# Attention probabilities turned by VectorE in 32x32 blocks, values in eight tiles of TensorE: one layer of a hybrid backbone

## The chip, the cores and the metric

The kernel runs on one core of a Trainium2 chip. The core has five engines with instruction streams of their own: TensorE (PE: matmuls and, ahead of each, a weight load, PEld), VectorE (DVE), ScalarE (ACT), GpSimd (POOL) and SyncE (SP, which here only issues DMAs). They wait for one another through semaphores. An engine works through its stream in order, so an instruction that waits holds everything behind it on that engine. The metric is the device time of one execution in microseconds (us). A profile of one execution shows every instruction with start and duration.

## The reference

One layer for 128 context tokens and 512 latent tokens, width 1024, 16 query heads of 64 in 4 groups that each share one key and value head, all in float32. The part that matters here:

```python
q = rms_norm(q.reshape(B, N, N_HEADS, HEAD_DIM), p["q_norm"])
...
keys = jnp.concatenate([ctx_k, apply_axial_rope(k, rope_tabs)], axis=1)
vals = jnp.concatenate([ctx_v, v], axis=1)
...
s = jnp.einsum('bqkgd,btkd->bkgqt', qblk, k) * scale
p = jax.nn.softmax(s, axis=-1)
o = jnp.einsum('bkgqt,btkd->bqkgd', p, v)
```

Latent queries read 128 cached and 512 new keys (640 in all), context queries the 128 context keys. The rest of the layer (modulation "ada", projections, a gated convolution, two output products, a feed-forward part) surrounds this.

## The kernel before

Tokens lie in tiles of 128 rows. Large products are made of three float32r matmuls, high and low parts of both operands (mm3, L157 to L159); the high part of a weight is a rounded copy, the low part the difference ("cut"). [...]

**The loop.** The attention runs over four head groups g, and in each over nine steps i: step 0 takes the context queries with all four heads, steps 1 to 8 take one tile of 128 latent queries and two heads each. A step has these parts:

- scores (L589): twelve matmuls, the two heads side by side in two row tiles of 64 partitions, into two PSUM buffers of 1024 columns; three of these exist (tag s2), taken in a ring.
- maxima per head on VectorE (L727), multiplied by the query's norm factor (L729); exponential with row sum on ScalarE (L742); reciprocal on VectorE (L751); shares (probabilities) on GpSimd, one multiply for each head (L752).
- The probabilities of the step before are turned on TensorE, ten 128x128 transposes against an identity (L765), and copied out of PSUM by ScalarE or VectorE (L770).
- After two steps of the same head pair, the values (L789): ten matmuls, two column tiles at once, keys on the partitions, 256 query columns moving. The result leaves as a high part (AH, ScalarE, L794) and a low part (AL, VectorE, L795). The context step's values are L780.

**What fills the steps.** Between these parts TensorE projects the queries of later tiles (q_part, 24 matmuls of mm3, in two halves), VectorE and GpSimd rotate them (L517 to L525), ScalarE squares them (L529) and VectorE and GpSimd make the norm factors (L535 to L537). q_turn (L560) transposes a finished query tile; its high part goes to ScalarE (L563) and its low part to VectorE (L566). In some steps a product of the modulation weights (ada, L209; its sum is folded by VectorE, L230) is made, and the weights that come next are cut (CUTS; high on ScalarE L690, low on VectorE L693). In the last group the projection of a gate takes the place of the queries' (gate_part).

**What sets the order.** The order on each engine is that of the program text, written out by hand in the loop. SP's queue loads raw weights by a ring: each use of a piece lets the next be fetched. Small results (query projections, query turns, ada, values) use ps1: two tiles of one PSUM bank each, taken in turn. Each of them is its own tile, so that a writer waits only for the readers of that one.

Of the kernel before, what the change touches and what calls it, by code (L numbers as in the profile page):

```python
# [14 lines left out]
ALU = mybir.AluOpType  # L15
# [46 lines left out]
def trunk_layer(ctx, tc, x_prompt, x_sample, cache_k, cache_v, c, c_ctx, w_ada, b_ada, g_pre1, g_post1, g_pre2,  # L62
# [25 lines left out]
    psa = single.enter_context(tc.tile_pool(name="psa", bufs=2, side="right", space=bass.MemoryType.PSUM))  # L88
# [12 lines left out]

    def ps1():
        return psa.tile([128, 512], F32, tag="s1", name=nm("s1"), bufs=2)
# [84 lines left out]
    bct = dp.tile([64, 128], F32, name="bct")  # L188
    hd = dp.tile([NT, 128, D], F32, name="hd")
# [75 lines left out]
    with tc.tile_pool(name="pro", bufs=2) as pro, tc.manual_schedule(engines={mybir.EngineType.SP}):  # L265
# [122 lines left out]
        VV = kvp_.tile([128, 6, 256], F32, name="VV")  # L388
# [59 lines left out]
        for f in range(KT):  # L448
# [7 lines left out]
            if f == 2:  # L456
                nc.sync.dma_start(VV[:, 0, :], cache_v.rearrange("t h d -> t (h d)"))
# [51 lines left out]
    with tc.tile_pool(name="att", bufs=2) as at:  # L509
        def wide(shape, s="pr"):  # L510
            return at.tile(shape, F32, tag="pr", name=nm(s), bufs=4)
# [30 lines left out]
        def q_begin(g):  # L542
            rq[g] = at.tile([128, NT, 4], F32, tag="rq", name=nm("rq"), bufs=2)

            QH[g], QL[g] = (at.tile([128, 2, NTOK], F32R, tag=x, name=nm(x), bufs=2) for x in ("QH", "QL"))
# [11 lines left out]
        def q_turn(g, t, p=None):  # L557
            p = ps1() if p is None else p
            for i in range(2):
                PE.transpose(p[:, i * 128:(i + 1) * 128], qfs[g, t][:, 2 * i:2 * i + 2].rearrange("p h d -> p (h d)"), ident)  # L560
            src = p[:, 0:256].rearrange("p (i c) -> p i c", i=2)
            qh, ql = (x[g][:, :, t * 128:(t + 1) * 128] for x in (QH, QL))
            S.activation(qh, src, AF.Copy)  # L563

            def low():
                V.tensor_tensor(out=ql, in0=src, in1=qh.bitcast(F32), op=ALU.subtract)  # L566
            return low

        def q_turn_both(g):

            p = ps2()
            for t in range(2):
                for i in range(2):
                    PE.transpose(p[:, 512 * t + i * 128:512 * t + (i + 1) * 128], qfs[g, t][:, 2 * i:2 * i + 2].rearrange("p h d -> p (h d)"),
                                 ident)
            src = p.rearrange("p (t i c) -> p i t c", t=2, c=128)[:, 0:2]
            qh, ql = (x[g][:, :, 0:256].rearrange("p i (t c) -> p i t c", t=2) for x in (QH, QL))

            def parts():
                S.activation(qh, src, AF.Copy)  # L580
                V.tensor_tensor(out=ql, in0=src, in1=qh.bitcast(F32), op=ALU.subtract)
            return parts

        def scores(outs, g, pi, qs, kh, kl, ks):

            for n, (kk, q) in enumerate(((kh, QH[g]), (kl, QH[g]), (kh, QL[g]))):
                for h in range(2):
                    rows = slice(64 * h, 64 * h + 64)
                    PE.matmul(outs[h], q[rows, pi, qs], kk[rows, g, ks], start=n == 0, stop=n == 2, tile_position=(64 * h, 0))  # L589
# [11 lines left out]
        ring = ada_raws(0, 1) + [("u", 10), ("u", 11)] + ada_raws(1, 4) + [("u", 12)] + ada_raws(4, 5) + [("u", 13)] + ada_raws(5, 8)  # L601
        ring += [("u", 14)] + ada_raws(8, 9) + [("u", 15)] + ada_raws(9, 12) + [("u", 16)] + ada_raws(12, 15) + [("u", 17)]
        ring += ada_raws(15, 16) + [("u", 18)]
# [28 lines left out]
        def k_rotate(t):  # L632
            if t in (0, 2):
                room = wide([128, 2, NKV, HD], "room")
                kf, tm = room[:, 0], room[:, 1]
                kds[t] = wide([128, NKV, 2, HD], "room")
            else:
                room = at.tile([128, 5, 256], F32, tag="PT", name=nm("room"), bufs=3)
                kf, tm = (room[:, i, :].rearrange("p (h d) -> p h d", d=HD) for i in range(2))
                kds[t] = room[:, 2:4, :].rearrange("p a (b s d) -> p (a b) s d", s=2, d=HD)  # L640
# [4 lines left out]
        def k_copies(t):  # L645
            sqs[t] = squares(kvp[t][:, 0:256])
            S.activation(VV[:, 5 if t == 0 else t, :], kvp[t][:, 256:512], AF.Copy)
# [4 lines left out]
        def k_double(t):  # L652
# [6 lines left out]
            if t == 0:  # L659
                nc.sync.dma_start(new_v.rearrange("t h d -> t (h d)"), VV[:, 5, :])  # L660
# [20 lines left out]
        PT = {}  # L681

# [3 lines left out]
        def cut_hi(i):  # L686
# [4 lines left out]

            def low(a=0, b=1024):
                V.tensor_tensor(out=lo[:, a:b], in0=raw[:, a:b], in1=hi[:, a:b].bitcast(F32), op=ALU.subtract)  # L693
                if b == 1024:
                    ring_used(1)
            state["cut"].append(Unit((hi, lo), units[i][4]))
            return low

        class Step:


            def __init__(self, g, place=None):
                self.g, self.place = g, place
                self.ctx = place is None
                self.pr = {}
                if self.ctx:
                    p = ps2().rearrange("p (h i c) -> p h i c", h=2, c=128)
                    for i in range(2):
                        scores([p[:, h, i, :] for h in range(2)], g, i, slice(0, 128), KCH, KCL, slice(0, 128))
                    self.sc = p[:, :, 0:2, :].rearrange("p h i c -> p i h c")  # L710
                else:
                    qh, pi, qi = place
                    q0 = NCTX + qh * 256 + qi * 128
                    both = [ps2(), ps2()]
                    for b0, b1 in BLKS:
                        scores([x[:, OFF + b0:OFF + b1] for x in both], g, pi, slice(q0, q0 + 128), KH, KL, slice(b0, b1))
                    self.sc = [x[:, OFF:OFF + NTOK] for x in both]

            def most(self, h):
                if self.ctx:  # L720
                    self.mx = small("mxc", 4, 1)
                    V.tensor_reduce(out=self.mx.rearrange("p (i h) -> p i h", h=2), in_=self.sc, axis=AX.X, op=ALU.max, negate=True)
                    V.tensor_tensor(out=self.mx, in0=self.mx, in1=rq[self.g][:, 0, :], op=ALU.mult)
                    return
                qh, pi, qi = self.place
                mx = small("mx")
                V.tensor_reduce(out=mx, in_=self.sc[h], axis=AX.X, op=ALU.max, negate=True)  # L727
                rs = rq[self.g][:, 1 + 2 * qh + qi, 2 * pi + h:2 * pi + h + 1]
                V.tensor_tensor(out=mx, in0=mx, in1=rs, op=ALU.mult)  # L729
                self.pr[h] = (mx, rs)  # L730

            def exps(self, h):
                if self.ctx:
                    pr, self.sm = at.tile([128, 4, 128], F32, tag="pr", name=nm("pr"), bufs=4), small("smc", 4, 1)
                    for i in range(4):
                        S.activation(pr[:, i, :], self.sc[:, i // 2, i % 2, :], AF.Exp, bias=self.mx[:, i:i + 1],
                                     scale=rq[self.g][:, 0, i:i + 1], accum_out=self.sm[:, i:i + 1])
                    self.pr = pr
                    return
                mx, rs = self.pr[h]  # L740
                pr, sm = wide([128, NTOK]), small("sm")
                S.activation(pr, self.sc[h], AF.Exp, bias=mx, scale=rs, accum_out=sm)  # L742
                self.pr[h] = (pr, sm)

            def shares(self, h):
                if self.ctx:
                    V.reciprocal(self.sm, self.sm)
                    G.tensor_tensor(out=self.pr, in0=self.pr, in1=self.sm.unsqueeze(2).broadcast_to((128, 4, 128)), op=ALU.mult)
                    return
                pr, sm = self.pr[h]  # L750
                V.reciprocal(sm, sm)  # L751
                G.tensor_tensor(out=pr, in0=pr, in1=sm.broadcast_to((128, NTOK)), op=ALU.mult)  # L752
                self.pr[h] = pr

            def turned(self, h):

                p = ps2()
                if self.ctx:
                    for i in range(4):
                        PE.transpose(p[:, i * 128:(i + 1) * 128], self.pr[:, i, :], ident)  # L760
                    dst = PT[self.g, "c"] = at.tile([128, 4, 128], F32, tag="PT", name=nm("PT"), bufs=3)
                    return lambda: S.activation(dst, p[:, 0:512].rearrange("p (h c) -> p h c", c=128), AF.Copy)
                qh, pi, qi = self.place
                for k in range(5):
                    PE.transpose(p[:, k * 128:(k + 1) * 128], self.pr[h][:, k * 128:(k + 1) * 128], ident)  # L765
                if qi == 0:
                    PT[self.g, qh, pi, h] = at.tile([128, 5, 256], F32, tag="PT", name=nm("PT"), bufs=3)
                dst = PT[self.g, qh, pi, h][:, :, qi * 128:(qi + 1) * 128]
                src = p[:, 0:640].rearrange("p (k c) -> p k c", c=128)
                return lambda v=False: V.tensor_copy(dst, src) if v else S.activation(dst, src, AF.Copy)  # L770

        def values(g, pair=None):

            vcol = slice(g * HD, (g + 1) * HD)
            pv = ps1()
            if pair is None:
                pt = PT.pop((g, "c"))
                for h in range(4):
                    o = 64 * (h % 2)
                    PE.matmul(pv[o:o + 64, (h // 2) * 128:(h // 2) * 128 + 128], VV[:, 5, vcol], pt[:, h, :], start=True, stop=True,  # L780
# [1197 lines left out]
```

## Time and profile before

| what | us |
|---|---|
| median of 3 runs | 1136.38 |
| lowest and highest | 1134.15, 1136.91 |
| span of the profiled execution | 1134.1 |
| first latent scores of group 0 | 77.03 |
| values of step 4 of groups 0, 1, 2, 3 begin | 96.04, 145.90, 195.76, 245.30 |
| last values of the attention | 278.9 to 281.3 |

TensorE is busy for 1114.9 us of the span (98%), VectorE for 796.3, ScalarE for 569.9 and GpSimd for 158.9. In the profile "busy" adds the durations of an engine's instructions; matmuls are pipelined, so their ends are modelled. A group of instructions is told by its line, engine, operation and tiles ("out<-in"), with count, busy time and the mean in ns, and behind the bar the idle time just ahead of them with what ended it. The chain of waits is the list of pieces followed back from the end: each is what released the next. The profile's lines bear the kernel's line numbers (L765), and "128*64" is the shape of the tile of TensorE's array. The attention stretch is about 206 us of the 1134.1; what comes after it (convolution, output and feed-forward products, mostly L1030) is the same text in both kernels.

### The profile page before, as it was taken

To read this page: it belongs to the slowest core of one execution; us is meant where nothing else is said; L and a number is where in the kernel's file an instruction comes from. 1 tells how busy PE (TensorE), PEld (TensorE's weight loads), DVE (VectorE), ACT (ScalarE), POOL (GpSimd) and SP (SyncE) were. 2 spreads that over 40 slices of the span, in tenths; PEclk is the share of its full clock that TensorE was granted. 3 is DMA by queue.
4 is the path that set the end of the run, shared out by engine and by line. 5 is a ranking of instruction groups with operands and counts; after the bars stand their busy time and mean duration, and the time that the engine had idled before them with its cause. 6 is when DMAs were issued, how large, how long until landed. Compare 5 with 4: busy or idle time off the path is not lost.

```text
span 1134.1 us, 19512 instructions
## 1 busy us (share of the span) xinstructions
PE 1114.9 (98%) x7885; PEld 1024.5 (90%) x7885; DVE 796.3 (70%) x1269; ACT 569.9 (50%) x979; POOL 158.9 (14%) x198
## 2 busy tenths in 40 slices
PE   7999999999999999999999999999999999999997
PEld 6787888888999999999999889999999999998786
DVE  4587666654656798889645458888788778888544
ACT  4375666665234444545522256655554545555431
POOL 2056566652000000000000012000000000002001
PEclk9999999999999999999999999999999999999999
DMA  9632433333222223223332644233333323315732
GB/s 335 205 92 82 126 94 112 110 96 112 76 75 75 75 77 105 81 75 95 93 111 76 207 164 150 76 99 99 98 112 109 95 91 109 105 61 186 240 99 93
DMA packets 177304, 129.58 MB, mean 114 GB/s; under 512 B 6274, under 2 KB 159422, under 8 KB 177214
## 3 DMA queue, kind: packets, MB, share of 16 engines
q1 hardware_dynamic: 177102, 128.30, 36.4%
q8 instruction: 62, 1.02, 0.4%
q14 instruction: 28, 0.23, 0.1%
q10 hardware_dynamic: 112, 0.04, 0.0%
HBM read 116.87 MB, written 11.45 MB: 113 GB/s over the span
## 4 chain that ended last, share of the span: by engine, by line
PE 89%; DVE 3%; ACT 1%; POOL 0%; issue 0%; DVEq 0%; POOLq 0%; ACTq 0%
PE b L1030 45%; PE b L159 9%; PE b L157 9%; PE b L158 9%; PE s L789 3%; PE s L765 3%; PE s L589 3%; PE s L157 2%; PE s L159 2%; PE s L158 2%; PE s L209 1%; DVE Y L1514 1%; DVE wlo L693 0%; PE s L560 0%; PE b L1421 0%; DVE mx L727 0%
## 5 line engine op out<-in xcount | busy, mean ns | idle before, releaser
L1030 PE MATMUL b<-ZB,whi 128*128 128x322 f32 x1024 | 228.6, 310 | 0.0
L1030 PEld LDWEIGHTS b<-ZB,whi 128*128 128x128 f32 x1024 | 173.8, 189 | 1.6
L1030 PE MATMUL b<-ZB,wlo 128*128 128x322 f32 x512 | 159.4, 311 | 0.0
L1030 PE MATMUL b<-MT,whi 128*128 128x320 f32 x608 | 134.1, 308 | 0.0
L1030 PEld LDWEIGHTS b<-MT,whi 128*128 128x128 f32 x608 | 101.7, 188 | 0.0
L1030 PEld LDWEIGHTS b<-ZB,wlo 128*128 128x128 f32 x512 | 96.2, 188 | 0.0
L1030 PE MATMUL b<-MT,wlo 128*128 128x320 f32 x304 | 93.8, 308 | 0.0
L752 POOL TENSOR_TENSOR pr<-pr,sm 128x640 f32<-128x640 f32 x64 | 80.7, 1270 | 61.1 <-DVE sm L751 61.1
L1017 ACT ACTIVATE whi<-SUM 128x1024 fp32r<-128x1024 f32 x40 | 42.2, 1055 | 79.6 <-DVE SUM L1484 77.2
L1514 DVE SCALAR_TENSOR_TENSOR Y<-C,cffn,Y 128x642 f32<-128x642 f32 x88 | 80.8, 920 | 0.9
L742 ACT ACTIVATE pr<-s,mx,rq 128x640 f32<-128x640 f32 x64 | 56.7, 886 | 38.5 <-DVE mx L729 36.4
L132 DVE TENSOR_TENSOR wlo<-raw,whi 128x1024 fp32r<-128x1024 f32 (+1 forms) x32 | 34.9, 1090 | 52.3 <-ACT whi L131 51.8
L1030 PE MATMUL b<-UH,whi 128*128 128x320 f32 x228 | 70.5, 309 | 0.0
L1030 PE MATMUL b<-UL,whi 128*128 128x320 f32 x228 | 70.4, 309 | 0.0
L1030 PE MATMUL b<-UH,wlo 128*128 128x320 f32 x228 | 70.2, 308 | 0.0
L1021 DVE TENSOR_TENSOR wlo<-raw,whi 128x1024 fp32r<-128x1024 f32 (+1 forms) x51 | 50.4, 1019 | 25.2 <-ACT whi L1017 24.3
L1017 ACT ACTIVATE whi<-WB 128x1024 fp32r<-128x1024 f32 x38 | 40.1, 1056 | 54.8 <-DVE WB L1125 54.8
L157 PE MATMUL s<-whi,UH 128*128 128x256 f32 (+1 forms) x200 | 65.8, 329 | 0.5 <-ACT UH L376 0.4
L727 DVE TENSOR_REDUCE mx<-s 128x1 f32<-128x640 f32 x64 | 52.5, 820 | 17.5 <-PE s L589 17.2
L158 PE MATMUL s<-wlo,UH 128*128 128x256 f32 (+1 forms) x200 | 61.5, 308 | 2.2 <-DVE wlo L693 2.2
L1038 ACT ACTIVATE p<-b 128x322 f32<-128x322 f32 (+1 forms) x78 | 34.3, 439 | 58.2 <-PE b L1030 58.2
L159 PE MATMUL s<-whi,UL 128*128 128x256 f32 (+1 forms) x200 | 61.8, 309 | 0.3
(322 smaller groups left out, 2933.0 us busy)
## 6 DMA issues: line engine op xcount, KB each, us to landing
raw<-in_w_in_dram SPq DMA_DIRECT2D x48, 512.0 KB, 3.6
RAW<-in_w_up_dram SPq DMA_DIRECT2D x40, 512.0 KB, 3.8
raw<-in_w_ada_dram SPq DMA_DIRECT2D x32, 512.0 KB, 4.0
raw<-in_w_down_dram SPq DMA_DIRECT2D x22, 512.0 KB, 4.2
actd<-Y SPq DMA_DIRECT2D x18, 321.0 KB, 2.5
AFB<-actd SPq DMA_DIRECT2D x18, 321.0 KB, 6.8
XT<-in_w_ada_dram SPq DMA_DIRECT2D x9, 512.0 KB, 8.5
raw<-in_w_conv_out_dram SPq DMA_DIRECT2D x9, 512.0 KB, 4.1
```

What stands on the lines that cost most here:

```text
L132: eng.tensor_tensor(out=lo[:, :n], in0=raw, in1=hi[:, :n].bitcast(F32), op=ALU.subtract)
L157: PE.matmul(out, ah, bh, start=start, stop=False)
L158: PE.matmul(out, ah, bl, start=False, stop=False)
L159: PE.matmul(out, al, bh, start=False, stop=stop)
L727: V.tensor_reduce(out=mx, in_=self.sc[h], axis=AX.X, op=ALU.max, negate=True)
L742: S.activation(pr, self.sc[h], AF.Exp, bias=mx, scale=rs, accum_out=sm)
L752: G.tensor_tensor(out=pr, in0=pr, in1=sm.broadcast_to((128, NTOK)), op=ALU.mult)
L1017: S.activation(to[0], raw, AF.Copy)
L1021: V.tensor_tensor(out=lo, in0=raw, in1=hi.bitcast(F32), op=ALU.subtract)
L1030: PE.matmul(out, p[:, ws], q[:, k, :], start=start and k == 0 and n == 0, stop=stop and k == 3 and n == 2, skip_group_check=True)
L1038: S.activation(t, pair[j][b], AF.Copy)
L1514: V.scalar_tensor_tensor(out=y, in0=crows(j)[i][:, d:d + NACT], scalar=cffn[:, 44 * d + o:44 * d + o + 1], in1=y, op0=ALU.mult, op1=ALU.add)
```

## The change

The probabilities are no longer turned by TensorE. VectorE transposes them in 32x32 blocks (one instruction for both heads of a step, 128 x 1280 elements), SBUF to SBUF, into a standing tile PT of six slots. A block transpose leaves the 128 queries of a tile in four quadrants of partitions and puts the keys of each block on the 32 partitions of that quadrant. So the values are made quadrant by quadrant: for each of 20 blocks of 32 keys and each of 4 quadrants and 2 heads one matmul with 32 keys on the partitions and 64 columns moving (32 queries of both head pairs): 160 matmuls for a step pair, in eight tiles of 32x64. The value rows are needed four times over, once for each quadrant of partitions; they go to DRAM (vd) and come back in that form (v_load), into regions that are free at the time (AL, KH, KL; the context's into AH).

Other parts: values at steps 1, 4, 6 and 8, query projections undivided at 0, 2, 3, 5 and 7; ada at 0, 1, 6 and 8; ps1 gives the two halves of one tile S1, which the values take whole (two quadrants in it, two in a buffer of s2); the multiply of the maximum goes from VectorE to a small ScalarE copy; the low parts of cut weights go from VectorE to GpSimd; one reciprocal for both heads; the gate's third block goes behind the loop.

```diff
-    psa = single.enter_context(tc.tile_pool(name="psa", bufs=2, side="right", space=bass.MemoryType.PSUM))
+    psa = single.enter_context(tc.tile_pool(name="psa", bufs=1, side="right", space=bass.MemoryType.PSUM))
...
+    S1 = psa.tile([128, 1024], F32, name="s1")
+    s1_next = [0]
+
     def ps1():
-        return psa.tile([128, 512], F32, tag="s1", name=nm("s1"), bufs=2)
+        s1_next[0] ^= 1
+        return S1[:, 512 * (1 - s1_next[0]):512 * (2 - s1_next[0])]
...
+        VR = [quads(x) for x in (AL[:, 4:6], AL[:, 6:8], KH[:, 0:2], KL[:, 0:2])]
...
+        def v_load(dst, src):
+            for i in range(4):
+                nc.sync.dma_start(dst[32 * i:32 * i + 32], src.rearrange("(c a) d -> a c d", a=32))
+
+        def v_group(g):
+            v_load(VR[g], vd[0:NTOK, g * HD:(g + 1) * HD])
...
             S.activation(hi, raw, AF.Copy)
-
-            def low(a=0, b=1024):
-                V.tensor_tensor(out=lo[:, a:b], in0=raw[:, a:b], in1=hi[:, a:b].bitcast(F32), op=ALU.subtract)
...
+            G.tensor_tensor(out=lo, in0=raw, in1=hi.bitcast(F32), op=ALU.subtract)
...
+                mx, low = small("mx"), small("mr")
+                V.tensor_reduce(out=mx, in_=self.sc[h], axis=AX.X, op=ALU.max, negate=True)
+                rs = rq[self.g][:, self.t, 2 * self.pi + h:2 * self.pi + h + 1]
+                S.activation(low, mx, AF.Copy, scale=rs)
+                S.activation(self.pr[:, h, :], self.sc[h], AF.Exp, bias=low, scale=rs, accum_out=self.sm[:, h:h + 1])
 
-            def shares(self, h):
+            def shares(self):
+                V.reciprocal(self.sm, self.sm)
...
+            def turned(self):
+
+                dst = CT.rearrange("p h c -> p (h c)") if self.ctx else flat[:, self.slot]
+                V.transpose(dst, self.pr.rearrange("p h c -> p (h c)"))
...
+            def out(self, i, h, a):
+                return self.p[i // 2][64 * h:64 * h + 64, 512 * (i % 2) + a:512 * (i % 2) + a + 64]
...
+            def pair(self):
+                s0 = 2 * ((4 * self.g + self.t - 1) % 3)
+                for c in range(20):
+                    for i in range(4):
+                        rows = slice(32 * i, 32 * i + 32)
+                        for h in range(2):
+                            PE.matmul(self.out(i, h, 64), VR[self.g][rows, c, :], PT[rows, s0:s0 + 2, h, 32 * c:32 * c + 32],
+                                      start=c == 0, stop=c == 19, tile_position=(32 * i, 64 * h))
...
+        CUTS = {(0, 1): 10, (0, 4): 11, (1, 1): 12, (1, 4): 13, (2, 1): 14, (2, 4): 15, (3, 1): 16, (3, 4): 17}
+        VALUES = {1: (-1, 4), 4: (0, 1), 6: (0, 2), 8: (0, 3)}
...
+                qt = asked({0: (g, 2), 2: (g, 3), 3: (g, 4), 5: (g + 1, 0), 7: (g + 1, 1)}.get(i))
+                first = asked({0: (g, 1), 2: (g, 2), 5: (g, 4), 7: (g + 1, 0)}.get(i))
...
+                if first:
+                    low = q_turn(*first)
+                if i in VALUES and (g or i > 1):
+                    v = Values(g + VALUES[i][0], VALUES[i][1])
+                    if v.t == 1:
+                        v.own()
+                    v.pair()
                 for h in range(1 if st.ctx else 2):
-                    st.most(h)
                     st.exps(h)
...
+                if low:
+                    low()
...
+                last.turned()
                 if qt:
                     pz = ps1()[:, 0:256]
-                    q_part(pz, *qt, range(4))
+                    q_part(pz, *qt, range(KT))
...
+                if i in (1, 6, 8) or (i == 0 and g):
+                    keep = ada_use(n_ada, S1[:, 256:384] if v else None)
+                    n_ada += 1
+                if v:
+                    v.high()
+                st.shares()
+                if v:
+                    v.low()
+                if keep:
+                    keep()
+                if (g, i) in CUTS:
+                    cut_hi(CUTS[g, i])
...
+                if i == 3:
+                    q_turn(g, 3)()
```

Two places of the changed order, both in step 5 of group 1, which has no values of its own but a query turn and a query projection. The first is VectorE's order before: the maxima of two heads with their multiplies, the low part of the turned query (L566), a reciprocal for each head, the low part of the next turn, and the rotation of the step's projection.

```order
L727 TENSOR_REDUCE mx_2869<-s_529_2851 128x1 [waits PE_49]
L729 TENSOR_TENSOR mx_2869<-mx_2869,rq_1674 128x1 [waits DVE_49]
L727 TENSOR_REDUCE mx_2875<-s_530_2852 128x1 [waits PE_49]
L729 TENSOR_TENSOR mx_2875<-mx_2875,rq_1674 128x1 [waits DVE_49]
L566 TENSOR_TENSOR QL_1676<-s_531_2865,QH_1675 128x2x128 [waits Activation_49]
L751 RECIPROCAL sm_2873<-sm_2873 128x1 [waits Activation_49]
L751 RECIPROCAL sm_2879<-sm_2879 128x1 [waits Activation_49]
L566 TENSOR_TENSOR QL_2437<-s_540_2918,QH_2436 128x2x128 [waits Activation_49]
```

The same place of the changed kernel (its line numbers are its own: L738 maximum, L589 low part of the turned query, L754 block transpose, L744 reciprocal, L537 the rotation's place for a context tile):

```order
L738 TENSOR_REDUCE mx_2691<-s_298_2671 128x1 [waits DVE_49,PE_49]
L738 TENSOR_REDUCE mx_2696<-s_299_2672 128x1 [waits DVE_49,PE_49]
L589 TENSOR_TENSOR Q_2689<-s_72,Q_2689 128x256 [waits Activation_49]
L754 STREAM_TRANSPOSE PT<-pr_2448 128x1280 [waits Pool_49]
L744 RECIPROCAL sm_2686<-sm_2686 128x2 [waits Activation_49]
L537 TENSOR_TENSOR qf_2731<-s_72,tabq 128x256 [waits PE_49]
```

The transpose of the step before, which waits for GpSimd's shares, now stands ahead of the step's reciprocal. The second place is TensorE's order there, after the scores: before,

```order
L560 MATMUL s_531_2865<-ident,qf_2722 128x128 [waits DVE_49]
L560 MATMUL s_531_2865<-ident,qf_2722 128x128
L157 MATMUL s_538_2882<-whi_2394,UH 128x256 [waits DVE_49]
L158 MATMUL s_538_2882<-wlo_2395,UH 128x256
L159 MATMUL s_538_2882<-whi_2394,UL 128x256
```

and in the changed kernel (L583 query turn, L161 to L163 query projection, s_72 is S1):

```order
L583 MATMUL s_72<-ident,qf_2422 128x128 [waits DVE_49,Pool_49]
L583 MATMUL s_72<-ident,qf_2422 128x128
L161 MATMUL s_72<-whi_2290,UH 128x256 [waits DVE_49]
L162 MATMUL s_72<-wlo_2291,UH 128x256
L163 MATMUL s_72<-whi_2290,UL 128x256
```

The first matmul of the projection waits for VectorE in both. Before, the semaphore count it waits for is reached by the fold of the ada product of the step before (L230, the bank's last reader); in the changed kernel it is reached by the subtraction L589 of this very step, which reads S1's other half.

More of the change, by code (lines that the diff above doesn't have):

```diff
@@ L571, in q_turn_both, with scores @@
             p = ps2()
[L572 to L586, printed above, removed]
+            return [q_turn(g, t, p[:, 512 * t:512 * t + 512]) for t in range(2)]
+        def scores(outs, g, t, pi, kh, kl, ks):
+            for n, (kk, q) in enumerate(((kh, QH[g, t]), (kl, QH[g, t]), (kh, QL[g, t]))):
                 for h in range(2):
                     rows = slice(64 * h, 64 * h + 64)
-                    PE.matmul(outs[h], q[rows, pi, qs], kk[rows, g, ks], start=n == 0, stop=n == 2, tile_position=(64 * h, 0))
+                    PE.matmul(outs[h], q[rows, pi, :], kk[rows, g, ks], start=n == 0, stop=n == 2, tile_position=(64 * h, 0))
         q_begin(0)
@@ L714, in __init__ @@
+                    self.t = 1 + n // 2
+                    self.slot = 2 * ((4 * g + n // 2) % 3) + n % 2
                     both = [ps2(), ps2()]
                     for b0, b1 in BLKS:
-                        scores([x[:, OFF + b0:OFF + b1] for x in both], g, pi, slice(q0, q0 + 128), KH, KL, slice(b0, b1))
+                        scores([x[:, OFF + b0:OFF + b1] for x in both], g, self.t, self.pi, KH, KL, slice(b0, b1))
                     self.sc = [x[:, OFF:OFF + NTOK] for x in both]
[L719 to L730, printed above, removed]
@@ L849, in trunk_layer @@
         last.exps(0)
-        last.shares(0)
+        last.shares()
+        v_group(1)
         def third(pz=pz):
@@ L887, in trunk_layer @@
[L887 to L899 removed]
+                if low:
+                    low()
@@ L905, in trunk_layer @@
                     pz = ps1()[:, 0:c1 - c0]
-                    gate_part(pz, c0, c1, range(4))
-                st.shares(0)
-                for f in after1:
-                    f()
-                copy = last.turned(0)
-                if last.ctx:
-                    copy()
-                else:
-                    copy(i == 2 or (qt is None and blk is None))
-                for f in late_hi:
-                    f()
-                if qt:
-                    q_part(pz, *qt, range(4, KT - 2 if start else KT))
@@ L955, in trunk_layer @@
-                if qt and not start:
-                    def rotation(pz=pz, qt=qt):
-                        q_rotate(pz, *qt)
-                        sq = squares(pz)
-                        after2.append(lambda: factors(sq, rq[qt[0]][:, qt[1], :]))
-                    if i == 2:
-                        after1.append(rotation)
-                    else:
-                        rotation()
+                    gate_part(pz, c0, c1, range(KT))
+                for f in after:
+                    f()
@@ new lines, in trunk_layer @@
+                after = []
+                keep = None
+                if i in (1, 6, 8) or (i == 0 and g):
[10 more added lines that the diff above has]
+                    cut_hi(CUTS[g, i])
+                if qt:
+                    q_rotate(pz, *qt)
+                    sq = squares(pz)
+                    after.append(lambda sq=sq, qt=qt: factors(sq, rq[qt[0]][:, qt[1], :]))
@@ L977, in trunk_layer @@
         fetch(20)
-        gate1_part(0, range(4))
+        gate1_part(0, range(KT))
         ada2_fold(acc)
-        last.turned(0)(True)
+        pz = ps1()[:, 0:128]
+        gate_part(pz, 512, NTOK, range(KT))
+        last.turned()
+        S.activation(gate0[:, 512:NTOK], pz, AF.Copy)
         S.activation(warm, mhalf[:, 0:1], AF.Sigmoid)
         cut_upto(19)
-        gate1_part(0, range(4, KT))
-        last.turned(1)()
         gate1_part(1, range(4))
-        hi, lo = values(NKV - 1, 3)
-        hi()
-        lo()
+        v = Values(NKV - 1, 4)
+        v.pair()
+        v.high()
+        v.low()
         gate1_part(1, range(4, KT))
```

234 lines of the change are left out of this document (86 added, 148 removed).

## Prediction

> **What bounds the kernel now.** I read the windows first, cut where the values of step 4 of each head group begin (96.04, 145.90, 195.76, 245.30 us), because the attention is the only stretch that the change edits.
>
> ```profile
> span 1134.1 us, 19512 instructions
> ...
> core 0: us, PE busy (x) PEld busy (x) DVE busy (x) ACT busy (x) POOL busy (x), PEclk, DMA share, GB/s
> 77.03:96.04 19.01, 15.60 (x133) 13.19 (x134) 15.63 (x37) 12.82 (x29) 12.86 (x13) 1.00 0.20 55
> 96.04:145.90 49.86, 49.86 (x540) 41.74 (x542) 33.44 (x91) 32.58 (x70) 30.69 (x32) 1.00 0.36 107
> 145.90:195.76 49.86, 49.86 (x540) 41.71 (x542) 33.44 (x91) 32.55 (x70) 30.68 (x32) 1.00 0.35 106
> 195.76:245.30 49.54, 49.54 (x540) 41.60 (x542) 32.00 (x88) 31.69 (x69) 30.67 (x32) 1.00 0.34 98
> ```
>
> The reader is to see that in the three periods TensorE (PE) is busy for all of it at granted clock 1.00, while the other engines have about 17 to 19 us of slack in 49.86. So there time is PE work, and only what leaves PE is gained. In the opening (77.03 to 96.04) PE idles 19.01 - 15.60 = 3.4 us. The chain of waits of one period, by line and in its first pieces, then the opening's longest piece, then a tail piece:
>
> ```profile
> by line: PE s L589 19.9%; PE s L789 19.2%; PE s L765 18.4%; PE s L157 10.8%; PE s L159 9.6%; PE s L158 9.5%; PE s L209 8.1%; PE s L560 2.8%; PE s L780 1.2%; PE s L760 1.2%
> 145.90 2.31 PE s L789 x20
> 148.21 1.24 PE s L765 x10
> 149.45 1.01 PE s L209 x32
> 150.46 1.08 PE s L589 x11
> 151.54 0.37 PE s L560 x2
> 151.91 0.12 PE s L157
> ...
> 87.11 3.47 DVE wlo L693 x2
> ...
> 276.63 0.55 PE s L765 x5
> ```
>
> Of 49.86 us, L765 (transposed probabilities) is 18.4% = 9.17, L760 (the same for context) 0.60, L789 (values) 9.57, L780 (context values) 0.60. The opening waits 3.47 us for two VectorE cuts of weights.
>
> **Values in eight tiles.** Before, a pair of heads takes ten matmuls, 20 records, in 2.31 us: two tiles side by side, ten records of 256 columns each. Now four row tiles by two column tiles do 160 matmuls, 320 records; per tile that is 40 records of 64 columns, 2560 columns as before. If all eight run together the price V stays 2.31. The rows that speak on it:
>
> ```profile
> L789 PEld LDWEIGHTS s<-PT,VV x84: 132/137/137, 145.8 to 195.7; 128*64 128x64 f32 x84
> L209 PEld LDWEIGHTS s<-raw,s x128: 106/110/110, 149.4 to 182.7; 128*32 128x32 f32 x128
> 149.38 0.81 PEld L209 LDWEIGHTS s<-raw,s 128*32 128x32 f32 x32 [0.17 <-issue]
> 156.56 0.31 PE L589 MATMUL s<-KH,QH 64*128 64x320 f32 x2
> 156.71 0.31 PE L589 MATMUL s<-KL,QH 64*128 64x320 f32 x2
> ```
>
> The last two show two row tiles running together. The third shows four column tiles in eight rounds of 0.10 us, which fits either loads that overlap behind 128 moving columns or four loads of 32 columns in a row. A load grows by 137 - 110 = 27 ns for 32 columns, so 64 columns are 54 ns of loading. If the loads of the two column tiles follow one another, a round costs 108 ns and 40 rounds 4.3 us. I take the middle of 2.31 and 4.3, V = 3.3, since the ada row leaves both open. Step 4's context values are eight more rounds, a fifth of V, so a group has 4.2 V = 13.9 where 9.57 + 0.60 stood.
>
> [...]
>
> **What leaves PE.** 9.17 + 0.60 + 9.57 + 0.60 = 19.94 goes, 13.9 comes: PE work per period 49.86 - 19.94 + 13.9 = 43.8 us, 6.0 less.
>
> **New waits on PE.** The two one-bank tiles become one tile S1 with two halves. In the order of the changed kernel, the first query-projection matmul of step 5 waits for VectorE behind the subtraction L589, though that reads the other half; the subtraction stands behind both maxima. Steps 2 and 7 are alike. The prices:
>
> ```profile
> 157.20 0.82 DVE L727 TENSOR_REDUCE mx<-s 128x1 f32<-128x640 f32 x1
> L727 DVE TENSOR_REDUCE mx<-s 128x1 f32<-128x640 f32 x17 | 14.0, 822 | 4.6 <-PE s L589 4.5
> L722 DVE TENSOR_REDUCE mxc<-s 128x4 f32<-128x512 f32 x1 | 0.7, 677 | 0.0
> L566 DVE TENSOR_TENSOR QL<-s,QH 128x256 fp32r<-128x256 f32 x5 | 2.1, 421 | 3.4 <-ACT QH L563 3.4
> L742 ACT ACTIVATE pr<-s,mx,rq 128x640 f32<-128x640 f32 x16 | 14.2, 887 | 8.7 <-DVE mx L729 8.5
> L742 ACT ACTIVATION_READ_ACCUMULATOR pr<-s,mx,rq 128x1 f32 x16 | 3.1, 192 | 0.0
> L529 ACT ACTIVATE sq<-s 128x256 f32<-128x256 f32 x5 | 1.9, 387 | 1.0 <-DVE qf L524 1.0
> ```
>
> Scores end; two maxima 1.64, the subtraction 0.42 and two hand-overs 0.1 make 2.17 us, of which PE fills 0.37 with the query turn: 1.8 us of waiting, three times, 5.4. In step 0 the maximum is 0.68 with a 0.16 multiply: 1.37 - 0.37 = 1.0. In step 3 the query turn waits for ScalarE's squares of the step's projection, which stand behind both exponentials: maximum 0.82, then twice (scaling 0.2, priced as the accumulator row, exponential 0.89, accumulator 0.19), squares 0.39 and hand-overs 0.2, 3.97 us after the scores, against 24 matmuls x 0.12 + switch = 2.9: 1.05. For the query turns behind an ada product, whose fold on VectorE now stands behind a transpose, I allow 0.5 three times, 1.5 (below: nothing). Together 9.0 us, so a period is 43.8 + 9.0 = 52.8, +2.9 on before. All ada and value products also write S1; their DMAs (the ring's half-megabyte pieces) keep their count.
>
> **VectorE and GpSimd.** VectorE loses the copies L770 and the multiplies L729, GpSimd gains the eight weight cuts. What matters is the new circle: shares on POOL, block transpose on DVE, then the next step's reciprocal behind it in DVE's order, then its shares.
>
> ```profile
> L752 POOL TENSOR_TENSOR pr<-pr,sm 128x640 f32<-128x640 f32 x17 | 21.2, 1255 | 15.0 <-DVE sm L751 15.0
> L537 POOL TENSOR_TENSOR rq<-ssq,mhalf 128x4 f32<-128x4 f32 x5 | 5.1, 1016 | 0.4
> L536 POOL TENSOR_SCALAR ssq<-ssq 128x4 f32<-128x4 f32 x5 | 1.8, 365 | 0.4
> L535 DVE TENSOR_REDUCE ssq<-sq 128x4 f32<-128x256 f32 x5 | 2.1, 412 | 0.4 <-ACT sq L529 0.4
> L770 DVE COPY PT<-s 128x640 f32<-128x640 f32 x4 | 3.3, 825 | 2.5 <-PE s L765 2.5
> L751 DVE RECIPROCAL sm<-sm 128x1 f32<-128x1 f32 x16 | 2.5, 159 | 3.2 <-ACT pr L742 3.2
> ```
>
> No transpose on DVE is in the trace. Nearest is the copy: 1280 columns at its rate are 1.65 us; half of that if it streams faster, double (3.3) if both passes of an element count. I take 1.65. A step's circle is 1.65 + 0.16 + 2 x 1.255 + 0.18 of hand-overs = 4.5; eight of them 36.0, the context step about 2.1, five steps with query factors inside 5 x 1.85 = 9.2, and a cut twice delays the shares by about 1.2: 49.7. That lies under 52.8 and costs nothing; without this cover (a slower transpose) it is the period. The reload of v by 16 small DMAs on SP's queue runs while PE has 50 us a group, and DMA is a third busy in the windows: nothing.
>
> **Sum.** Three periods 3 x 2.9 = +8.7. From 245.30 on: five steps' transposes off PE, ten times 0.55 = -5.5; four pairs at V, +4.0; one wait 1.8 (step 5): +0.3. The third gate block only moves behind the loop. Opening: the 3.47 wait goes, but new ones of POOL's cut and the exponentials come: half of it, -1.6. Sum +7.4 on the profiled 1134.1 us: 1141.5. The median of the shown runs lies 2.3 above that span: **1144 us**.
>
> **Rivals.** *Faster.* PE's new waits are covered and V is 2.31: PE work 49.86 - 19.94 + 9.7 = 39.6, waits 6.4 without the allowance and the squares, period 46.0 if the transpose takes half the copy's rate; 3 x -3.9, -5.5 + 1.8 and -3.2 make 1118, and halfway to no change 1127. It decides once 4.2 V plus the waits fall under 19.9. For it: equal columns per tile; against: the waits are in the order. *Tiles don't run together* (the change then doesn't do what it says): with serial loads V = 4.3, period 57.0, 3 x 7.1 + 4.3 - 1.6 gives 1160; with records issued no faster than the third row's mean, 0.81 / 32 = 25 ns, V = 8.1, period 72.9, 3 x 23.1 + 19.5 - 1.6 gives 1224. For it: 640 instructions a pair; against: pairs that start together. *The circle sets the pace:* transpose at 3.3, 49.7 + 8 x 1.65 = 62.9 per period, 3 x 13.0 + 1 - 1.6 gives 1175. For it: reciprocal behind the transpose; against: the copy's rate.
>
> **How the numbers follow.** Forecast 0.44, own range 1136 to 1158 (V from 2.8 to 4.0); faster 0.25; serial loads 0.14; V near 8, 0.07; circle 0.10. A measurement here can tell 0.3% (3.4 us) from no change: 1133.0 to 1139.8 gets 0.09 from the forecast's low side and 0.02 from the faster case. Slower 0.35 + 0.14 + 0.07 + 0.10 = 0.66, faster 0.23. The range 1126 to 1180 leaves out half the faster case, V near 8 and part of the circle, some 0.2 in all.
>
> **What would show it.** In the new profile: L781 in the chain (320 records a pair; 2.3, 3.3 or 4.3 us); idle PE before L161 in steps 2, 5, 7 released by DVE Q L589, 1.8 us each; PE busy near 44 of 53 us a period; STREAM_TRANSPOSE near 1.65 us; POOL not above nine tenths busy. If PE idle lies before L781 and is released by DVE's transpose, the circle ruled; if PE is never idle and the period below 48, the faster case did.

## The result

The changed kernel takes 1272.66 us (median of 4 runs, 1267.71 to 1279.97) against 1136.63 for the kernel before; the ratio is 1.1207, 95% interval 1.1165 to 1.1249. The forecast was 1144 us with a range of 1126 to 1180. One execution of experiment 4's kernel took 1415.24 us at a granted clock of 0.733 where its other three took 1219.79 to 1224.34, and it is left out of the times below.

The page of the changed kernel begins so (the second line is the granted TensorE clock in forty slices, the third the queue that brings instructions, with packets, MB and share):

```profile
span 1267.9 us, 28884 instructions
...
PEclk9977886787778899999999999999999999999999
...
q8 instruction: 98, 1.61, 0.5%
```

The same lines of the kernel before:

```profile
PEclk9999999999999999999999999999999999999999
...
q8 instruction: 62, 1.02, 0.4%
```

The reader is to see two new things. The clock, 0.9 or more in every slice before, falls to digits of 6 to 8 tenths in slices 3 to 14, the attention. And 98 packets of instructions of 16 KB each were fetched where the kernel before fetched 62. The windows, cut where the values of step 4 of each group begin, as before the change:

```profile
core 0: us, PE busy (x) PEld busy (x) DVE busy (x) ACT busy (x) POOL busy (x), PEclk, DMA share, GB/s
77.00:114.41 37.41, 24.20 (x218) 20.95 (x223) 18.59 (x39) 16.89 (x46) 15.67 (x16) 0.68 0.31 82
114.41:189.46 75.05, 54.91 (x1735) 47.97 (x1725) 36.92 (x72) 29.36 (x76) 33.49 (x32) 0.86 0.25 73
189.46:273.79 84.33, 61.85 (x1736) 54.01 (x1725) 37.01 (x72) 29.27 (x76) 34.30 (x34) 0.76 0.30 80
273.79:355.80 82.01, 61.55 (x1735) 53.43 (x1725) 37.19 (x73) 29.19 (x76) 34.99 (x35) 0.76 0.23 67
...
417.00:1267.00 850.00, 841.90 (x5185) 799.25 (x5184) 613.70 (x794) 400.06 (x618) 23.07 (x44) 1.00 0.34 107
```

What follows the attention takes 850 us (851 before, from 283 on); the attention itself went from 206 to 340 us (77 to 417), which is the whole difference of 134. A period of 49.86 us became 75, 84 and 82. PE is busy for 62 of 84 us: no longer the work, and more than the 43.8 us that the prediction gave it. The waits of PE in the second period (engine and line, what it waited for, us in all, times, longest):

```profile
PE s L781 <- issue: 13.1, 7, 2.7
PE s L161 <- DVE Q L589: 5.5, 4, 1.6
PE s L583 <- ACT sq L549: 1.6, 1, 1.6
PE s L214 <- issue: 1.6, 1, 1.6
```

The second and third line are the waits at the shared tile that the prediction worked out (6.4 and 1.05 us). The first and the last, 14.7 us, were not foreseen: "issue" is time in which PE waited for nothing that the profile shows. The chain of waits around one pair's values shows where that time lies:

```profile
207.73 1.08 PE s L602 x12
208.81 2.23 PE s L781 x131
211.04 1.97 issue
213.01 1.85 PE s L781 x93
214.86 0.57 PE s L214 x4
215.43 1.58 issue
217.01 1.92 PE s L214 x28
218.93 1.94 PE s L602 x12
...
220.90 0.70 issue
221.60 0.81 DVE mx L738
222.42 0.34 DVE Q L589
...
222.81 0.38 PE s L161
```

Scores (L602, 1.08 us at full clock) are followed by value records at a fast pace, then nothing for 2 us, then records again, and a second hole in the middle of the ada product L214. Behind them the same ada and score work takes nearly twice as long (ada 1.92 us for 28 records, before 1.01 for 32; scores 1.94): half clock, which the trace's clock records give from 213.9 to 220.7 us. Then comes the wait at the shared tile. The DMA view of this stretch, 207 to 219 us in forty slices of 0.3 us, has three packets in all:

```profile
GB/s 0 0 0 0 0 0 0 0 0 0 0 55 0 0 0 0 0 0 0 0 0 0 0 55 0 0 0 0 0 0 0 0 0 0 0 0 0 55 0 0
DMA packets 3, 0.05 MB, mean 4 GB/s; under 512 B 0, under 2 KB 0, under 8 KB 0
...
q8 instruction: 3, 0.05, 1.8%
```

They begin at about 210.3, 214.0 and 218.1 us, 3.7 to 4.1 us apart, and PE starts again at 213.0 and 217.0, some 2.7 to 3 us after a fetch began. By the counts a packet of 16 KB goes with about 256 of PE's instructions, 128 records with their weight loads: its 25251 instructions in the trace over 98 packets are 258 each, and before 15918 over 62 are 257. Numbering PE's instructions in the order of their starts shows 28 holes of over 0.9 us, from one start to the next, at one place of a block of 256: 25 of them ahead of a value matmul and 3 in the ada product (time, number modulo 256, hole in ns; eight of the 28 in a row):

```
213.0  193  2182
217.0  193  1999
232.8  193  2383
237.1  193  2914
256.0  193  2352
277.1  193  1870
280.8  193  2362
295.1  193  2085
```

The 28 holes make 58.0 us. The other stretches of over 0.9 us in the attention stand at other places of a block and at other lines (L161 most often), where PE waits for another engine. Last, the two new instructions themselves, from the views of their lines:

```profile
L781 PE MATMUL s<-PT,AL x2560: 211/233/365, 114.4 to 256.7; 32*64 32x64 f32 x197
...
L754 DVE STREAM_TRANSPOSE PT<-pr x32: 1501/1502/1514, 103.8 to 402.1; 128x1280 f32<-128x1280 f32 x32
```

### The profile page after: what moved, and what is told of

Its sections match the earlier page's. It is cut to its first block, busy times and chain, and to the rows that moved or that the text cites. A ratio compares the mean times of both kernels' runs of the same rounds, so it can differ in the third digit from the quotient of the medians.

```text
span 1267.9 us, 28884 instructions
## 1 busy us (share of the span) xinstructions
PE 1157.9 (91%) x12573; PEld 1069.7 (84%) x12573; DVE 808.0 (64%) x1194; ACT 557.7 (44%) x1005; POOL 173.5 (14%) x206
## 4 chain that ended last, share of the span: by engine, by line
PE 85%; issue 5%; DVE 5%; ACT 2%; DMA 1%; POOL 1%; SPq 0%; DVEq 0%; POOLq 0%; ACTq 0%
PE b L1004 40%; PE b L163 8%; PE b L161 8%; PE b L162 8%; PE s L781 5%; PE s L602 4%; PE s L161 3%; PE s L163 3%; PE s L162 3%; PE s L214 2%; DVE mx L738 1%; DVE Y L1488 1%; DMA XT<-in_w_ada_dram 1%; DMA XT<-in_x_sample_dram 0%; ACT pr L741 0%
## 5 line engine op out<-in xcount | busy, mean ns | idle before, releaser
L161 PE MATMUL s<-whi,UH 128*128 128x256 f32 (+1 forms) x200 | 73.1, 366 | 22.1 <-DVE Q L589 17.7
L161 PEld LDWEIGHTS s<-whi,UH 128*128 128x128 f32 x200 | 46.0, 230 | 31.2 <-DVE Q L589 21.6
L163 PE MATMUL s<-whi,UL 128*128 128x256 f32 (+1 forms) x200 | 69.5, 347 | 0.4
L162 PE MATMUL s<-wlo,UH 128*128 128x256 f32 (+1 forms) x200 | 69.1, 346 | 0.0
L799 DVE TENSOR_TENSOR AL<-s,AH 128x128 fp32r<-128x128 f32 (+1 forms) x32 | 9.9, 324 | 92.2 <-ACT AH L794 92.2
L738 DVE TENSOR_REDUCE mx<-s 128x1 f32<-128x640 f32 x64 | 49.8, 820 | 21.5 <-PE s L602 21.5
```

The costliest lines, as they stand in the source:

```text
L161: PE.matmul(out, ah, bh, start=start, stop=False)
L162: PE.matmul(out, ah, bl, start=False, stop=False)
L163: PE.matmul(out, al, bh, start=False, stop=stop)
```

## The experiments

The theory after reading the trace (F): PE uses up the instructions of the many small matmuls faster than they are fetched. With it (K): idle stretches of PE bring its granted clock down to half (0.5 in the clock records), so that each costs more than itself. Its rivals: the array does the eight tiles in turn (M), or the shared tile's waits make most of it (S).

**1. The same matmuls with 2 moving columns.**

```diff
-                            PE.matmul(self.out(i, h, 64), VR[self.g][rows, c, :], PT[rows, s0:s0 + 2, h, 32 * c:32 * c + 32],
+                            w = 32 if c == 0 else 1
+                            dst = self.out(i, h, 64).rearrange("p (k b) -> p k b", k=2)[:, :, 0:w]
+                            PE.matmul(dst, VR[self.g][rows, c, :], PT[rows, s0:s0 + 2, h, 32 * c:32 * c + w],
```

> The same 160 value matmuls per step pair, but from the second key block on they move 2 columns instead of 64 (this leaves out most of the probability columns). In the changed kernel's trace PE's value records start 11 to 17 ns apart in blocks, and after each block of 128 records (256 instructions with their weight loads, 16 KB, the size of one packet of the instruction queue) PE idles 1.2 to 2.9 us put down to issue. Theory F (supply of instructions): count and place of the gaps stay, a pair still takes 6 to 9 us, total 1255 to 1275. Rival M (array work: the eight tiles don't run together): the work falls to about a twentieth, a pair takes under 3.5 us, total under 1210.

Measured: 1282.87 us in one run. The chain of waits of one pair (L783 are the values here):

```profile
214.57 1.97 PE s L783 x113
216.54 1.80 issue
218.34 1.90 PE s L783 x124
220.24 0.57 PE s L214 x4
220.81 0.98 issue
```

With a twelfth of the columns (102 of 1280 a tile) a pair still takes 5.3 to 9.0 us, and 25 holes of 53.6 us stand at the same place where 28 of 58.0 stood. M falls: the moving columns don't set the time. The total lies above F's own range of 1255 to 1275: 228 us of its attention passed at half clock by the trace's clock records, 154 in the changed kernel. The weight loads are as many as before, so this experiment alone doesn't rule them out; that the holes lie at one place of a block of 256 does.

**2. Two key blocks of twenty.**

```diff
-                for c in range(20):
+                for c in range(2):
...
-                                      start=c == 0, stop=c == 19, tile_position=(32 * i, 64 * h))
+                                      start=c == 0, stop=c == 1, tile_position=(32 * i, 64 * h))
```

> Only two of 20 key blocks are multiplied (16 matmuls, 32 records per step pair; the other keys are left out of the values). Theory F: no idle time of PE after blocks of 128 records, a pair under 0.6 us, and a period between the values of step 4 of two groups falls from 82 us to that of the circle shares, block transpose, reciprocal: 48 to 52 us; total 1125 to 1145. For the clock: theory K (the granted clock falls wherever PE has idle stretches of 1 to 2 us, whatever their cause) expects it to stay below 0.9 in the periods although no instruction is late; rival K2 (only the gaps of late instructions bring it down) expects 1.00.

Measured: 1178.31 us in one run. One period in the windows (columns as above):

```profile
182.20:243.20 61.00, 47.79 (x568) 40.52 (x566) 37.40 (x71) 28.32 (x76) 34.18 (x33) 0.72 0.45 109
```

and PE's longest waits in it:

```profile
PE s L161 <- DVE Q L589: 5.1, 4, 1.5
PE s L602 <- ACT pr L741: 3.8, 6, 0.9
PE s L583 <- ACT sq L549: 1.8, 1, 1.8
```

The window runs from the values of step 6 to those of the next step 6. Nine tenths of the value instructions are gone, no hole at a block's end is left, and 94 us went with them, but the total misses F's range of 1125 to 1145 and the period its 48 to 52: the clock stands at 0.72 although no instruction is late. PE waits 13 us in the period, in stretches of up to 1.8 us, and that is enough. K2 falls. The value work here is a tenth, so the period also shows that the rest of the change, with the shared tile, would not reach the 49.86 us of before.

**3. S1 as two tiles of a bank each.** The copies of the results follow (not shown).

```diff
-        s1_next[0] ^= 1
-        return S1[:, 512 * (1 - s1_next[0]):512 * (2 - s1_next[0])]
+        return psa.tile([128, 512], F32, tag="s1", name=nm("s1"), bufs=2)
...
-                self.p = [ps2(), S1]
+                x = ps2()
+                self.p = [x[:, 0:512], x[:, 512:1024], ps1(), ps1()]
```

> S1 is two tiles of one bank again, as before the change; the values take both, and their results leave in four pieces each instead of two. The trace of the changed kernel puts 5.5 us of PE's idle time in a period of 84 down to VectorE's low part L589 and 1.9 to ScalarE's squares. Theory F: these go, the gaps of instructions stay: 3 to 8 us less in a period, total 1235 to 1262. Rival S (the waits at the shared tile, through the lower clock that they bring, make most of the loss): period under 65, total under 1200.

Measured: 1221.93 us, ratio to the kernel before 1.0781 (1.0749 to 1.0813). One period in the windows, from step 6 to step 6:

```profile
181.50:254.30 72.80, 56.26 (x1719) 49.92 (x1717) 37.11 (x79) 29.64 (x84) 33.49 (x34) 0.81 0.35 93
```

and PE's waits in it (L778 are the values):

```profile
PE s L778 <- issue: 15.1, 7, 3.5
PE s L778 <- ACT sq L545: 0.6, 2, 0.4
```

The waits at the tile are gone to 0.4 us and less and the issue holes stay, as F expects. But the gain is 51 us where F expected 11 to 38, and S isn't reached either. The values of step 4 begin at 98.3, 166.0, 239.0 and 308.6 us here, so the three periods of 75, 84 and 82 us became 67.7, 73.0 and 69.6: some 7 us of waits in each were worth 7 to 12, and half-clock time went with them (154 us of half clock in the attention of the changed kernel by the trace's clock records, 102 here). Another 16 us come from the opening, in which the values of step 4 began at 114.4.

**4. Half as many matmuls for the same columns.** Values for two query tiles at once, at steps 6 and 1; the slots of the probabilities and the copies of the results follow (not shown).

```diff
-                            PE.matmul(self.out(i, h, 64), VR[self.g][rows, c, :], PT[rows, s0:s0 + 2, h, 32 * c:32 * c + 32],
+                            PE.matmul(self.out(i, h, 64), VR[self.g][rows, c, :], PT[rows, s0:s0 + 4, h, 32 * c:32 * c + 32],
...
-        VALUES = {1: (-1, 4), 4: (0, 1), 6: (0, 2), 8: (0, 3)}
+        VALUES = {1: (-1, 2), 6: (0, 1)}
```

> The values are made for two query tiles at once, twice in a group (at steps 6 and 1): 128 moving columns instead of 64, half the matmuls, the same columns through the array. Theory F: half of the instructions, eight pairs instead of sixteen with gaps after blocks of 128 records, 6 to 8 us each: 45 to 65 us less with part of the clock regained, total 1200 to 1225. Rival M (array work): no change, 1260 to 1280.

Measured: 1221.63 us (median of three), ratio 1.0762 (1.0739 to 1.0785): 51 us less, as F has it. The packets fall from 98 to 78 and the holes at block ends from 28 to 16, 58.0 to 28.2 us. M expected no change. The weight loads are halved with the matmuls; what ties the loss to the fetching of instructions and not to them is the place of the holes.

**5. Both edits.** The edits of 3 and 4 together.

> Both edits together: 128 moving columns (half the value matmuls) and S1 as two tiles. Theory F+K (late instructions and shared-tile waits both stop PE, and both bring the granted clock down): the two gains of about 50 us add up, total 1160 to 1190, clock in the periods over 0.9. Rival (they cover one another, since a wait hides behind a late block): the second gain is mostly lost, total 1205 to 1225.

Measured: 1176.62 us, ratio 1.0365 (1.0335 to 1.0395). The gain of both is 96 us, of the 102 that the two make by themselves: they hardly cover one another. The clock is 0.92, 0.89 and 0.94 in the three periods, where over 0.9 was expected.

**6. Few key blocks and two tiles.** The edits of 2 and 3 together; 18 of 20 key blocks are left out of the values.

> Two of 20 key blocks (the values of the other keys are left out) with S1 as two tiles: neither late instructions nor waits at the shared tile. With the shared tile the same cut gave 1178 us, a period of 57 to 61 and a clock of 0.72 in it. Theory K: PE's idle time in a period falls from 13 us to under 5, the clock comes back to over 0.95, the period to that of the circle shares, transpose, reciprocal, 46 to 51 us, total 1120 to 1145. Rival: the scores' waits for the exponentials (3.8 us in that period) and the circle keep PE idle, the clock stays under 0.85, total over 1160.

Measured: 1129.07 us in one run; a gain of 144 us, again the sum of the two (94 and 51). The three periods:

```profile
96.29:143.10 46.81, 37.72 (x573) 31.90 (x573) 37.42 (x80) 28.69 (x84) 32.85 (x33) 0.93 0.38 114
143.10:194.93 51.83, 41.42 (x574) 35.11 (x574) 37.83 (x80) 28.74 (x84) 34.31 (x35) 0.84 0.52 128
194.93:241.24 46.31, 37.72 (x574) 32.07 (x574) 37.42 (x80) 28.78 (x84) 33.84 (x34) 0.93 0.40 115
```

The total and two of the three periods came out as expected. The clock didn't come back to 0.95, and PE's idle time is 9 to 10 us a period, not under 5: PE still waits for the exponentials (3.7 us in the second period) and for raw ada weights (3.8 us). So with values nearly free and no wait at S1 the change would be worth some 6 us, although the transposes (four times 9.17, or 37 us) and most of the value work are gone from PE. Little of the time that left PE left the kernel. The chain of waits of the first period has at its head the shares on GpSimd (14.7%), a load of raw weights (13.2%) and the block transposes (11.2%).

**7. One part alone: the cuts on GpSimd.** In the kernel before, the low parts of units 10 and 11.

```diff
-                V.tensor_tensor(out=lo[:, a:b], in0=raw[:, a:b], in1=hi[:, a:b].bitcast(F32), op=ALU.subtract)
+                (G if i < 12 else V).tensor_tensor(out=lo[:, a:b], in0=raw[:, a:b], in1=hi[:, a:b].bitcast(F32), op=ALU.subtract)
```

> One part of the change alone in the kernel before: the low parts of the first two weight cuts in the loop on GpSimd instead of VectorE, where they stand in a chain of waits with 3.47 us. If that part was worth what the prediction gave the opening (1.6 us): 1133 to 1136 us, ratio 0.997 to 1.000. Rival: GpSimd takes 2.4 us for each and its shares come later, no gain, ratio 1.000 to 1.003.

Measured: 1135.66 us, ratio 1.0008 (0.9999 to 1.0018): the same time. Moving the cuts off VectorE brought nothing; the chain of the opening now runs over GpSimd's shares and its cuts (2.44 and 1.23 us in their longest pieces). What the 3.47 us wait would be worth without that load on GpSimd is not shown.

**8. One part alone: the wait.** In the kernel before, query turn and projection of steps 0 and 5 in one bank.

```diff
+                    room = ps1()
-                    low1.append(q_turn(*first))
+                    low1.append(q_turn(*first, room))
...
-                    pz = ps1()[:, 0:256]
+                    pz = room[:, 256:512] if first else ps1()[:, 0:256]
```

> In the kernel before, the query turn and the query projection of steps 0 and 5 share one bank, so the projection waits for VectorE's low part there: the new wait alone, about 1.8 us twice in a period (1.2 in step 0), nothing else changed. If such waits cost only themselves: about 3 us a period, 1144 to 1150 us, clock 1.00. Theory K (an idle stretch of PE near 2 us brings the granted clock down for a window of 3.4 us or more): clock under 0.97 in the periods and 1155 to 1180 us.

Measured: 1153.25 us, ratio 1.0150 (1.0132 to 1.0167), between the two expectations. The first period in the windows:

```profile
95.95:152.95 57.00, 53.21 (x539) 44.61 (x538) 33.53 (x91) 32.69 (x70) 30.69 (x32) 0.94 0.31 94
```

and PE's only wait in it:

```profile
PE s L157 <- DVE QL L566: 3.8, 2, 2.0
```

The period grew by 7.1 us: 3.8 of waiting, and 3.35 by which PE's own work got longer (53.21 for 49.86) at a clock of 0.94. Two stretches of half clock of 3.4 us stand in the trace of this period. So a wait of 1.9 us costs about 3.6 here, and this without any late instruction. The second period has one such stretch and grew by 5.7 us for the same 3.8 of waiting.

## Why the prediction failed, step by step

- **What bounded the kernel** (PE work, all of it) was right, and so was that the rest of the kernel is untouched.
- **The step that failed** is "I take the middle of 2.31 and 4.3, V = 3.3". A pair took 5.6 to 9.2 us from its first start to its last. The bounds came from the array and its weight loads; the trace has the value records 10.7 ns apart in their fast blocks. 320 of them would be 3.4 us, near the price taken; that the middle of two open bounds fell there is luck, since no row of the trace before spoke for it. Most of the rest is instruction blocks that come too late, 28 holes of 58.0 us, and half clock. Rivals spoke of "640 instructions a pair", but as an issue rate, not as bytes to be fetched. The signs were in the page of before: 62 packets of 16 KB on the instruction queue, four of them in a period of 49.86 us. The change brings some 13 in a period, most of them in four bursts. The place of the holes and experiments 1 and 4 show the cause: moving columns hardly matter, instructions do.
- **The case "records issued no faster than 25 ns"** came near in size (V = 8.1, 1224 us) by another mechanism: inside a block the records are twice as dense, and the time is lost between blocks. The 25 ns, which are the mean of one ada row of before (0.81 us over 32 loads), don't hold as a limit here, against 10.7 ns measured over eight tiles; at 10.7 ns a record each of the four row groups gets a load every 43 ns on average, while a matmul record lasts 211 ns and more (its end is modelled).
- **The waits at the shared tile** were right in place and length (5.5 us for four, forecast 6.4; 1.6 at step 3, forecast 1.05), and wrong in price: they were added at their own length. Experiment 8 shows that such a wait costs 1.5 to 1.9 times its length, experiment 3 that some 7 us of them a period were worth 7 to 12.
- **The clock** was no term at all. The first windows said 1.00 and the sum kept it, although the forecast itself put 9 us of idle time into each period. At a mean of 0.78 over 340 us, 75 us of full clock are missing, part of them in idle time.
- **The circle** of shares, transpose and reciprocal was priced well (the transpose took 1.50 us, forecast 1.65), and in the changed kernel it doesn't rule: GpSimd is busy 34 of 84 us. With the other two losses gone it is near the limit, since in experiment 6 the periods are 46.8, 51.8 and 46.3 us and the forecast had 49.7 for the circle. The forecast also took PE's work with its waits, or the circle, whichever is longer. For experiment 2 that would be 49.7 (work and waits 43.8 + 9.0, less nine tenths of 13.9, are 40.3), and its three periods took 56.6, 60.5 and 59.0 at clocks of 0.75 to 0.82. So the cover that the forecast counted on failed there; how much of it is the clock was not separated.
- **The opening** was to gain 1.6 us; 77 to 114.41 is 37.41 us where 19.01 stood, at a clock of 0.68. Experiment 7 shows that the cuts on GpSimd bring nothing by themselves. Most of the rest is the shared tile: with S1 as two tiles the values of step 4 begin at 98.3 us (experiment 3) and at 96.3 (experiment 6), against 114.4 in the changed kernel and 113.2 in experiment 2, which keeps the tile. The forecast had no wait at the tile in the opening.

The sum of the parts as the runs show it: nine tenths of the value instructions are worth 94 us (experiment 2: their work, the holes and the half clock that goes with them), of which the forecast's own price covers 50 (nine tenths of four times 13.9); the shared tile is worth 51 (experiment 3); both together 144 (experiment 6). The loss was 136, so everything else together, the transposes off PE among it, is a gain of some 6 to 8 us. No version tried beats the kernel before; the nearest that computes everything is experiment 5, 41 us behind. Values for a whole group at once, a quarter of the matmuls, were not tried; they would need two more slots of probabilities, 10 KB a partition.

## What to carry to other kernels

Count instructions as well as columns: where a change multiplies small matmuls, divide them into blocks of 256 instructions and set a few us (here 3.7 when they follow closely) against the time that PE needs for a block (here 1.37 in the fast ones); fewer and longer matmuls ease it, and here half as many took the holes from 58.0 to 28.2 us. Price a new wait of PE of one or two us above its length where PE was busy all the time before (here 1.5 to 1.9 times), and look for the granted clock in the windows first when a forecast puts idle time on PE. A tile with two halves is one tile to the semaphores: a writer of one half waits for readers of the other (here 5.5 us in a period at L161 for L589; with two tiles, in experiment 3, waits of 0.4 us and less were left).

## What the runs showed of the hardware

- **Instructions come in blocks.** PE ran through a block of 256 in 1.37 us (128 records, 10.7 ns apart) where it ran fast, and at the 28 holes of the changed kernel it started again 2.2 to 3.0 us after the begin of the last fetch. The packets (16 KB, 258 instructions each on average) and the place of the holes, 193 modulo 256, agree on blocks of 256; the holes make 58.0 us.
- **The clock answers to short idle stretches.** In experiment 8 six waits of 1.8 to 2.0 us brought five stretches of 3.4 us at half clock, each beginning 1.7 to 3.3 us after the start of a wait; the kernel before has none in its attention.
- **Eight tiles of 32x64 run side by side.** Their fp32 records are 10.7 ns apart in the fast blocks with 64 moving columns, about 9 with 2 (experiment 1) and about 14 with 128 (experiment 4). At one block of 128 records every 3.7 us the supply gives one record in 29 ns. The 160 matmuls of a pair stand in the trace as 320 records; in the kernel before the ten of a pair were 20, while the 80 transposes of a period (L765) were 80.
- **A transpose in 32x32 blocks** of 128 x 1280 float32 took 1.50 us on VectorE, 1.17 ns a column.
